# Fusing the layer-0 query, key and value units to 512 columns, with a new TensorE order, in a two-layer diffusion trunk

## The chip, the cores and the metric

The kernel runs on one core of one Trainium2 chip. The metric is the device time of one execution in microseconds (us); three executions of the kernel before gave a median of 1700.06 us, between 1699.44 and 1702.07.

## The reference, cut to what matters

The program is one inference step of a two-layer trunk. Layer 0 mixes tokens with differential attention, layer 1 with neighbourhood attention; each is followed by a squared-ReLU MLP. There are 128 context tokens and 512 latent tokens, 1024 features. The change touches only layer 0's mixer, which for the latent tokens is

```python
def diff_qkv(h, w_qkv):
    q, k, v = jnp.split(h @ w_qkv, 3, -1)        # 8 heads, each 2 x 64 of q and k, 128 of v
...
def diff_lat(h, ck, cv, w_qkv, lam, subln, w_o):
    q, k, v = diff_qkv(h, w_qkv)
    q, k = axial_rope(q), axial_rope(k)          # rotation, latent tokens only
    k_all = jnp.concatenate([ck, k], 1)          # 128 cached keys + 512 latent keys
    v_all = jnp.concatenate([cv, v], 1)
    # per head: p = softmax over 640 keys of two score maps; a = p0 - lam * p1; o = a @ v_all
    return diff_attend(q, k_all, v_all, diff_lambda(lam), subln) @ w_o
```

Context tokens do the same among themselves, without rotation. All matmuls of the projections are done in three passes of split numbers (high x high, low x high, high x low).

## The kernel before

Tokens are held in five tiles of 128 (`t` 0 to 3 latent, 4 context). The weights of the query, key and value projection lie in six chunks of 512 columns (chunk 0: v of heads 0 and 1, q and k of head 0; 1: q1 k1, v of heads 2 and 3; 2: q2 k2, q3 k3; 3: v of heads 4 and 5, q4 k4; 4: q5 k5, v of heads 6 and 7; 5: q6 k6, q7 k7). A chunk is four groups; a ring of five groups is kept in SBUF. When the last user of a group has run (`used`, `done`, the counts in `left`, L88 to L95), the next group is converted (`conv`: one ACT cast L194, two DVE subtractions L196) and a further load is issued on SP's queue (`pump`, three raw buffers, which also carry the modulation weights).

TensorE's instructions run in exactly the order of the string `ORDER0` (L40); the other engines are ordered by the compiler. Each name in it is one step:

- `q{i}{t}`, `v{i}{t}` (`unit0`, L525): the projection of one token tile to 256 columns: 8 k-tiles x 3 passes = 24 matmuls into one M bank (four PSUM banks M). `A` (`pair0`) does the q units of head 1 for two tiles together. `e{t}` takes head 0's parts out of the first stage's accumulators.
- `qk0_evac` (L481): takes a q unit out of PSUM. Latent tiles are rotated by four DVE instructions (L497 to L500) into a buffer `nt`, with a small ACT copy (L506). There are three buffers `nt` and one spare piece of the output tile `X`; the buffer is held until `r{i}{t}`. `v_evac` (L438): ACT cast and DVE subtraction (L126, L127) of a v unit.
- `r{i}{t}` (L515): three transposes of a buffer `nt`; ACT and DVE then write the queries (L517, L519) and keys (L518, L521). The queries have one buffer, so `r{i}{t}` comes after `S{i-1}{t}`.
- `S{h}{b}` (`scores0`): the scores of 128 queries of head h, 8 matmuls of 320 columns into two PSUM tiles S. There are just two such tiles; each is free again when its exponential has been taken. `softmax0`: per tile a DVE maximum (L570) and an ACT exponential (L572), then DVE L578 to L580 make one map E.
- `c{h}`: the context's scores, 4 matmuls, into one tile S, with the same softmax.
- `T{h}{b}` (L591): five transposes of E; at b = 1 a sixth, of the context's map (L593). `C{h}`, `P{h}`: the products with v (3 and 15 matmuls). `Q{h}` (L626): ten one-column matmuls for the mean square; after heads 3, 5, 6 and 7 a DVE and ACT chain of small instructions follows (`rstd0`, L637 to L646, with a table load for the square root), and `D3` and `D5` (L651) transpose its result.
- `m{g}`, `M{g}`: one modulation unit (8 weight tiles against the conditioning vector) and its two transposes.

```python
    def S(self):
        self.turn = (self.turn + 1) % len(self.psS)
        return self.psS[self.turn].tile([P, 1024], F32, tag="S", name=self.nm("S"))
...
        s2 = [self.S().rearrange("p (a b) -> p a b", b=512) for _ in range(2)]
        for hf in range(2):
            ks = slice(P + 320 * hf, P + 320 * hf + 320)
            self.qk([s2[m][:, hf, :320] for m in range(2)], self.q0, K, qs, lambda z: z[:, ks])
```

Of the kernel before, what the change touches and what calls it, by code (L numbers as in the profile page):

```python
# [39 lines left out]
ORDER0 = """  # L40
    e0 e4 A e2 v10 e1 m8 v13 b e3 r00 r04 q10 r02 q14 r01 q12 r03 m9 M8 S00 r10 v11 S01 r11 v12 c0 r14 v14 M9
    T00 S02 q21 q20 q30 r12 m10 T01 S03 r13 q23 m11 T02 S10 T03 r20 q31 C0 c1 M10 P0 m12 T10 S11 M11 r21 M12
    q22 S12 m13 q24 r22 T11 S13 r23 q32 r24 C1 T12 S20 r30 m14 M13 Q0 T13 M14 c2 P1 S21 T20 r31 q33 S22 T21
    q34 r32 Q1 S23 r33 v21 v20 r34 S30 T23 q40 v24 m15 T22 S32 C2 P2 m16 T30 r40 S31 q42 M16 q41 c3 r42 q43
    q44 T31 S33 r43 v22 r41 v23 M15 C3 r44 Q2 T32 q50 T33 S40 m17 P3 m18 S41 M18 q52 c4 Q3 T40 q51 v33 D3 r51
    r50 q53 M17 S42 v31 r52 q54 T41 S43 r54 r53 v30 S50 T43 v34 T42 v32 S51 q70 q61 C4 P4 c5 m19 T50 q60 m20
    M19 S52 r60 M20 q62 m21 r61 T52 q63 T51 S53 r62 M21 q64 r63 m22 r64 T53 C5 S60 M22 Q4 P5 S61 q71 m23 N2 c6
    Q5 M23 r70 q72 r71 T60 S62 D5 N1 T61 q73 N0 r72 q74 S63 N3 C6 T62 N4 N5 X r73 r74 o00 S70 T63 o02 c7 P6
    o03 T70 S71 Q6 o01 T71 D6 S72 o04 o10 T72 S73 C7 N6 o11 T73 o12 P7 o13 Q7 D7 o14 N7 j00 j10 j01 j11 g0 j12
    g1 j02 j13 h0 g2 j03 j04 h1 j14 g3 g4 h2 f0 f2 h3 f3 h4 f1  # L50
"""
# [14 lines left out]
class Net:  # L66
    def __init__(self, tc, a, o, stack):
# [22 lines left out]
        for l in range(2):  # L90
            for n in range(NCH):
                k = (9, 9, 8, 9, 9, 8)[n] if n < 6 and l else 10 if n < 6 else 8 if n > 7 and n % 4 < 2 else NTT
                for x in range(4):
                    self.left[4 * (NCH * l + n) + x] = k
# [17 lines left out]
    def op(self, name, fn, *needs):  # L112
        self.ops[name] = fn, needs
# [367 lines left out]
    def qk0_evac(self, pool, i, t, src):  # L481
        nc = self.nc
        if self.spare[1] not in self.ops:
            self.spare[1] = f"r{i}{t}"
            nt = self.spare[0][:, 0:384]
        else:
            nt = pool.tile([P, 384], F32, tag="nt", name=self.nm("nt"), bufs=3)
# [36 lines left out]

    def unit0(self, pool, kind, i, t, n, c):  # L525
        m = self.M()
        self.nat(self.h, t, n, m[:, :256], c, c + 256)
        if kind == "v":
            self.v_evac(pool, i, t, m[:, :256], "cv0", "v0")
        else:  # L530
            self.qk0_evac(pool, i, t, m[:, :256])

    def pair0(self, pool, ts):
        ms = [(t, self.M()[:, :256]) for t in ts]
        for k0, k1 in ((0, 6), (6, KT)):
            for t, m in ms:
                self.nat(self.h, t, 1, m, 0, 256, k0, k1, k0 == 0)
        for t, m in ms:
            self.qk0_evac(pool, 1, t, m)

# [132 lines left out]
    def layer0_attn(self, acc0):  # L673
        nc, a = self.nc, self.a
        with self.tc.tile_pool(name="at0", bufs=1) as pool:
# [5 lines left out]
            X = self.X([P, KT, NT])  # L681
            self.spare = [X[:, 6, :], "", ""]
            heads, norms, late = {}, {}, {}

# [53 lines left out]
            op("b", lambda: (self.banks("M", 4), self.lambdas(pool)), "e4")  # L738
            for kind, i, n, c in (
                ("q", 1, 1, 0), ("v", 1, 1, 256), ("q", 2, 2, 0), ("q", 3, 2, 256), ("v", 2, 3, 0), ("q", 4, 3, 256),  # L740
                ("q", 5, 4, 0), ("v", 3, 4, 256), ("q", 6, 5, 0), ("q", 7, 5, 256),
            ):
                for t in range(NTT):
                    if i == 1 and kind == "q" and t in A0:
                        continue
                    op(f"{kind}{i}{t}", lambda x=(kind, i, t, n, c): self.unit0(pool, *x))
            for g in range(KT, 24):
                op(f"m{g}", lambda g=g: self.mod_unit(pool, g))
            for h in range(8):
                rot = ("e",) if h == 0 else (f"q{h}",)  # L750
                for b in range(4):
                    op(f"S{h}{b}", lambda h=h, b=b: scores(h, b), *rot, f"r{h}")
                    op(f"T{h}{b}", lambda h=h, b=b: self.trans0(heads[h], b, b == 1), f"S{h}{b}", f"c{h}" if b == 1 else "-", f"T{h}0" if b else "-", f"P{h - 1}")
                op(f"c{h}", lambda h=h: self.ctx_scores0(heads[h]), *rot, f"r{h}", f"S{h}0")
                op(f"C{h}", lambda h=h: self.ctx_pv0(heads[h]), f"T{h}1", f"v{h // 2}4")
                op(f"P{h}", lambda h=h: pv(h), f"T{h}", f"v{h // 2}", f"C{h}")
                op(f"Q{h}", lambda h=h: ssq(h), f"P{h}")
                if h in (3, 5, 6, 7):
                    op(f"D{h}", lambda h=h: diag(h), *(f"Q{x}" for x in range(h + 1)))
                op(f"N{h}", lambda h=h: norm(h), f"D{max(h, 3 if h < 4 else 5)}", *(("X",) if h > 5 else ()))  # L760
            op("X", swap, "N0", "N1", "N2", "N3", "N4", "N5", "q", "v", "m", "M")
            first4 = self.proj_ops(pool, 0, late, EARLY0, "S73", ("N6", "N7"), ("E0", 2, "E1"))
# [638 lines left out]
```

## Time and profile before

| what | us |
|---|---|
| median of 3 executions | 1700.06 |
| the profiled execution | 1701.12 |
| its span in the profile | 1699.3 |
| layer 0's attention, from `A` (56.60) to `T50` (280.22) | 223.6 |
| TensorE busy, whole span | 1620.8 |
| VectorE busy, whole span | 1116.3 |
| ScalarE busy, whole span | 662.4 |

The profile's times are counted from the span's start. PE is the TensorE matmul, PEld its weight load, DVE VectorE, ACT ScalarE, POOL GpSimd, SP the queue that issues most transfers. In the timeline a row holds start, duration, engine, line of the kernel, operation, tile written <- tiles read, and in brackets the idle time of the engine just before it with what ended it. A matmul's duration includes its drain, so rows of PE overlap: what one matmul costs in a stream is the distance between two starts.

### The profile page before, as it was taken

To read this page: it belongs to the slowest core of one execution; us is meant where nothing else is said; L and a number is where in the kernel's file an instruction comes from. 1 tells how busy PE (TensorE), PEld (TensorE's weight loads), DVE (VectorE), ACT (ScalarE), POOL (GpSimd) and SP (SyncE) were. 2 spreads that over 40 slices of the span, in tenths; PEclk is the share of its full clock that TensorE was granted. 3 is DMA by queue.
4 is the path that set the end of the run, shared out by engine and by line. 5 is a ranking of instruction groups with operands and counts; after the bars stand their busy time and mean duration, and the time that the engine had idled before them with its cause. 6 is when DMAs were issued, how large, how long until landed. Compare 5 with 4: busy or idle time off the path is not lost. (4 is left out here: it accounts for less than half of the span.)

```text
span 1699.3 us, 25833 instructions
## 1 busy us (share of the span) xinstructions
PE 1620.8 (95%) x10026; PEld 1466.2 (86%) x10026; DVE 1116.3 (66%) x2121; ACT 662.4 (39%) x1338; POOL 370.3 (22%) x280
## 2 busy tenths in 40 slices
PE   8999999899999999999999999998899999999997
PEld 5788989787988988989888999997797898998996
DVE  4788778875668789798465777778655433242337
ACT  2466555743621221312335556565361122130321
POOL 2100000000062246164311001100015314334321
PEclk9999999999999999999999999999999999999999
DMA  8432334331424445353224443444042222122211
GB/s 335 131 133 93 100 116 151 112 130 40 162 86 149 161 137 185 125 186 124 88 86 160 126 126 119 148 149 168 15 148 74 79 71 85 65 85 65 89 61 62
DMA packets 61373, 200.73 MB, mean 118 GB/s; under 512 B 7764, under 2 KB 14402, under 8 KB 60226
## 3 DMA queue, kind: packets, MB, share of 16 engines
q1 hardware_dynamic: 55618, 175.09, 30.8%
q0 software_dynamic: 5632, 23.99, 4.1%
q8 instruction: 79, 1.29, 0.3%
q14 instruction: 44, 0.36, 0.1%
HBM read 186.41 MB, written 7.40 MB: 114 GB/s over the span
## 5 line engine op out<-in xcount | busy, mean ns | idle before, releaser
L194 ACT CAST wh<-rw 128x1024 fp32r<-128x1024 f32 x192 | 197.2, 1051 | 359.9 <-PE M L121 269.3
L121 PE MATMUL S<-hhi,wl 128*128 128x320 f32 (+1 forms) x944 | 292.7, 310 | 4.1 <-DVE wl L196 2.7
L119 PE MATMUL S<-hhi,wh 128*128 128x320 f32 (+1 forms) x944 | 292.0, 309 | 1.1 <-DVE tmp L1136 1.1
L120 PE MATMUL S<-hlo,wh 128*128 128x320 f32 (+1 forms) x944 | 291.5, 309 | 0.0
L196 DVE TENSOR_TENSOR wl<-rw,wh 128x512 fp32r<-128x512 f32 x278 | 247.9, 931 | 51.6 <-ACT wh L194 50.0
L196 POOL TENSOR_TENSOR wl<-rw,wh 128x512 fp32r<-128x512 f32 x106 | 182.2, 1738 | 405.7 <-ACT wh L194 404.1
L120 PE MATMUL M<-wl,uhi 128*128 128x512 f32 x640 | 252.2, 394 | 6.7 <-DVE wl L196 6.7
L119 PE MATMUL M<-wh,uhi 128*128 128x512 f32 x640 | 251.7, 393 | 1.8 <-ACT uhi L126 1.8
L121 PE MATMUL M<-wh,ulo 128*128 128x512 f32 x640 | 251.6, 393 | 0.3
L119 PE MATMUL M<-wh,hhi 128*128 128x256 f32 (+1 forms) x640 | 201.3, 314 | 8.2 <-DVE tmp L1136 3.2
L121 PE MATMUL M<-wh,hlo 128*128 128x256 f32 (+1 forms) x640 | 196.3, 307 | 5.2 <-DVE hlo L127 5.2
L120 PE MATMUL M<-wl,hhi 128*128 128x256 f32 (+1 forms) x640 | 195.6, 306 | 0.0
L121 PEld LDWEIGHTS S<-hhi,wl 128*128 128x128 f32 x944 | 178.4, 189 | 7.3 <-DVE wl L196 5.5
L119 PEld LDWEIGHTS S<-hhi,wh 128*128 128x128 f32 x944 | 178.5, 189 | 1.6 <-DVE tmp L1136 1.3
L120 PEld LDWEIGHTS S<-hlo,wh 128*128 128x128 f32 x944 | 178.4, 189 | 0.2
L120 PEld LDWEIGHTS M<-wl,uhi 128*128 128x128 f32 x640 | 121.4, 190 | 33.6 <-DVE wl L196 8.8
L119 PEld LDWEIGHTS M<-wh,uhi 128*128 128x128 f32 x640 | 121.4, 190 | 28.3 <-ACT uhi L126 3.6
L121 PEld LDWEIGHTS M<-wh,ulo 128*128 128x128 f32 x640 | 121.5, 190 | 26.9 <-DVE ulo L127 1.7
L293 DVE SCALAR_TENSOR_TENSOR jk<-wm,cb 128x1024 bf16<-128x1024 f32 x96 | 143.0, 1489 | 1.5
L119 PEld LDWEIGHTS M<-wh,hhi 128*128 128x128 f32 x640 | 124.1, 194 | 15.2 <-DVE tmp L1136 3.4
L121 PEld LDWEIGHTS M<-wh,hlo 128*128 128x128 f32 x640 | 123.6, 193 | 13.8 <-DVE hlo L127 9.3
L1195 DVE SCALAR_TENSOR_TENSOR r<-S,r 128x640 f32<-128x640 f32 (+1 forms) x62 | 48.4, 781 | 128.1 <-ACT r L1194 127.9
(278 smaller groups left out, 2958.7 us busy)
## 6 DMA issues: line engine op xcount, KB each, us to landing
rw<-in_w SPq DMA_DIRECT2D x192, 512.0 KB, 4.3
wm<-in_wmodT SPq DMA_DIRECT2D x48, 512.0 KB, 3.5
rw<-in_wmod SPq DMA_DIRECT2D x32, 512.0 KB, 4.4
E<-in_bias POOLq DMA_DIRECT2D x32, 384.0 KB, 5.4
wm<-in_wmod SPq DMA_DIRECT2D x8, 1024.0 KB, 10.7
Q<-Q SPq DMA_DIRECT2D x16, 320.0 KB, 4.1
gate<-gates POOLq DMA_DIRECT2D x6, 512.0 KB, 4.9
X<-in_xT SPq DMA_DIRECT2D x8, 320.0 KB, 11.4
```

Of the source, the lines that this page charges most:

```text
L119: te.matmul(out, sh, mh, start=start, stop=False)
L120: te.matmul(out, sh, ml, start=False, stop=False)
L121: te.matmul(out, sl, mh, start=False, stop=stop)
L194: keep(nc.scalar.copy(hi, r))
L196: keep(eng.tensor_tensor(lo[:, k], r[:, k], hi[:, k], ALU.subtract))
L293: op = nc.vector.scalar_tensor_tensor(jk, ws[t], 1.0, cb[:, x, :], ALU.mult, ALU.mult, accum_out=mc[:, t, x : x + 1])
L1195: nc.vector.scalar_tensor_tensor(rv, src, 0.0, rv, ALU.max, ALU.mult)
```

## The change

Query and value units that share a chunk become one unit of 512 columns: q1 with v1, q2 with q3, v2 with q4, q5 with v3, for each of the five token tiles; chunks 0 and 5 stay as they were. One M bank then holds both halves, and `evac0` takes them out one after the other. `A` computes 512 columns for tiles 1 and 3. Since head 3's rows are projected together with head 2's, long before they are transposed, their rotated rows are kept in three planes of the output tile `X` that are not yet in use (`nt3`) and not in the buffers `nt`. The counts of `left` follow (5 uses of a group in chunks 1 to 4). `ORDER0` is new up to `c5`; from `T50` on it is unchanged. The `v` names are gone from the rules. The diff:

```diff
--- before.py
+++ after.py
@@ -38,16 +38,15 @@
 HALF = (slice(0, 64), slice(64, 128))
 
 ORDER0 = """
-    e0 e4 A e2 v10 e1 m8 v13 b e3 r00 r04 q10 r02 q14 r01 q12 r03 m9 M8 S00 r10 v11 S01 r11 v12 c0 r14 v14 M9
-    T00 S02 q21 q20 q30 r12 m10 T01 S03 r13 q23 m11 T02 S10 T03 r20 q31 C0 c1 M10 P0 m12 T10 S11 M11 r21 M12
-    q22 S12 m13 q24 r22 T11 S13 r23 q32 r24 C1 T12 S20 r30 m14 M13 Q0 T13 M14 c2 P1 S21 T20 r31 q33 S22 T21
-    q34 r32 Q1 S23 r33 v21 v20 r34 S30 T23 q40 v24 m15 T22 S32 C2 P2 m16 T30 r40 S31 q42 M16 q41 c3 r42 q43
-    q44 T31 S33 r43 v22 r41 v23 M15 C3 r44 Q2 T32 q50 T33 S40 m17 P3 m18 S41 M18 q52 c4 Q3 T40 q51 v33 D3 r51
-    r50 q53 M17 S42 v31 r52 q54 T41 S43 r54 r53 v30 S50 T43 v34 T42 v32 S51 q70 q61 C4 P4 c5 m19 T50 q60 m20
-    M19 S52 r60 M20 q62 m21 r61 T52 q63 T51 S53 r62 M21 q64 r63 m22 r64 T53 C5 S60 M22 Q4 P5 S61 q71 m23 N2 c6
-    Q5 M23 r70 q72 r71 T60 S62 D5 N1 T61 q73 N0 r72 q74 S63 N3 C6 T62 N4 N5 X r73 r74 o00 S70 T63 o02 c7 P6
-    o03 T70 S71 Q6 o01 T71 D6 S72 o04 o10 T72 S73 C7 N6 o11 T73 o12 P7 o13 Q7 D7 o14 N7 j00 j10 j01 j11 g0 j12
-    g1 j02 j13 h0 g2 j03 j04 h1 j14 g3 g4 h2 f0 f2 h3 f3 h4 f1
+    e0 e4 A e2 e1 m8 b e3 r00 r04 q10 r02 r01 q14 r03 m9 M8 S00 r10 S01 r11 q12 c0 r14 M9 T00 S02 r12 q21 m10 T01
+    S03 r13 m11 T02 q20 S10 T03 r20 C0 c1 M10 P0 m12 T10 S11 M11 r21 M12 q22 S12 m13 T11 r22 q24 S13 r24 C1 T12 q23
+    Q0 m14 M13 T13 r23 S20 r30 M14 c2 P1 S21 T20 r31 q40 S22 T21 r32 Q1 S23 T22 r33 r34 q42 S30 T23 m15 C2 P2 m16
+    T30 r40 q41 S31 M16 c3 T31 r41 q43 S32 M15 r42 S33 C3 T32 q44 r43 Q2 T33 m17 r44 S40 P3 q50 m18 T40 S41 M18 r50
+    q51 c4 Q3 D3 T41 r51 S42 M17 q52 T42 r52 S43 q53 C4 r53 T43 q54 P4 m19 r54 S50 S51 q70 q61 c5 T50 q60 m20 M19
+    S52 r60 M20 q62 m21 r61 T52 q63 T51 S53 r62 M21 q64 r63 m22 r64 T53 C5 S60 M22 Q4 P5 S61 q71 m23 N2 c6 Q5 M23
+    r70 q72 r71 T60 S62 D5 N1 T61 q73 N0 r72 q74 S63 N3 C6 T62 N4 N5 X r73 r74 o00 S70 T63 o02 c7 P6 o03 T70 S71 Q6
+    o01 T71 D6 S72 o04 o10 T72 S73 C7 N6 o11 T73 o12 P7 o13 Q7 D7 o14 N7 j00 j10 j01 j11 g0 j12 g1 j02 j13 h0 g2 j03
+    j04 h1 j14 g3 g4 h2 f0 f2 h3 f3 h4 f1
 """
 ORDER1 = """
     e1 e3 e2 e0 b q03 v04 B00 q00 B03 q01 q02 q12 v11 S00 q10 B01 B02 c0 B10 q11 S01 v13 q13 B12 S02 T00 v12
@@ -89,7 +88,7 @@
         self.left = [0] * (8 * NCH)
         for l in range(2):
             for n in range(NCH):
-                k = (9, 9, 8, 9, 9, 8)[n] if n < 6 and l else 10 if n < 6 else 8 if n > 7 and n % 4 < 2 else NTT
+                k = ((10, 5, 5, 5, 5, 10), (9, 9, 8, 9, 9, 8))[l][n] if n < 6 else 8 if n > 7 and n % 4 < 2 else NTT
                 for x in range(4):
                     self.left[4 * (NCH * l + n) + x] = k
         self.left[: 4] = [NTT] * 4
@@ -480,7 +479,9 @@
 
     def qk0_evac(self, pool, i, t, src):
         nc = self.nc
-        if self.spare[1] not in self.ops:
+        if i == 3:
+            nt = self.nt3[:, 384 * t : 384 * t + 384]
+        elif self.spare[1] not in self.ops:
             self.spare[1] = f"r{i}{t}"
             nt = self.spare[0][:, 0:384]
         else:
@@ -522,21 +523,26 @@
 
         self.op(f"r{i}{t}", tr, f"S{i - 1}{t}" if t < 4 else f"c{i - 1}")
 
-    def unit0(self, pool, kind, i, t, n, c):
+    def unit0(self, pool, t, n, parts):
         m = self.M()
-        self.nat(self.h, t, n, m[:, :256], c, c + 256)
-        if kind == "v":
-            self.v_evac(pool, i, t, m[:, :256], "cv0", "v0")
-        else:
-            self.qk0_evac(pool, i, t, m[:, :256])
+        self.nat(self.h, t, n, m[:, : 256 * len(parts)], 256 * parts[0][2], 256 * parts[-1][2] + 256)
+        self.evac0(pool, t, m, parts)
+
+    def evac0(self, pool, t, m, parts):
+        for x, (kind, i, _) in enumerate(parts):
+            src = m[:, 256 * x : 256 * x + 256]
+            if kind == "v":
+                self.v_evac(pool, i, t, src, "cv0", "v0")
+            else:
+                self.qk0_evac(pool, i, t, src)
 
     def pair0(self, pool, ts):
-        ms = [(t, self.M()[:, :256]) for t in ts]
+        ms = [(t, self.M()) for t in ts]
         for k0, k1 in ((0, 6), (6, KT)):
             for t, m in ms:
-                self.nat(self.h, t, 1, m, 0, 256, k0, k1, k0 == 0)
+                self.nat(self.h, t, 1, m, 0, 512, k0, k1, k0 == 0)
         for t, m in ms:
-            self.qk0_evac(pool, 1, t, m)
+            self.evac0(pool, t, m, (("q", 1, 0), ("v", 1, 1)))
 
     def mod_unit(self, pool, g):
         acc = self.M()
@@ -680,6 +686,7 @@
             self.ssq = pool.tile([P, KT, NTT], F32, name="ssq")
             X = self.X([P, KT, NT])
             self.spare = [X[:, 6, :], "", ""]
+            self.nt3 = X[:, 3:6, :].rearrange("p a b -> p (a b)")
             heads, norms, late = {}, {}, {}
 
             def first(t):
@@ -736,29 +743,29 @@
                 op(f"e{t}", lambda t=t: first(t))
             op("A", lambda: self.pair0(pool, A0))
             op("b", lambda: (self.banks("M", 4), self.lambdas(pool)), "e4")
-            for kind, i, n, c in (
-                ("q", 1, 1, 0), ("v", 1, 1, 256), ("q", 2, 2, 0), ("q", 3, 2, 256), ("v", 2, 3, 0), ("q", 4, 3, 256),
-                ("q", 5, 4, 0), ("v", 3, 4, 256), ("q", 6, 5, 0), ("q", 7, 5, 256),
+            for i, n, parts in (
+                (1, 1, (("q", 1, 0), ("v", 1, 1))), (2, 2, (("q", 2, 0), ("q", 3, 1))), (4, 3, (("v", 2, 0), ("q", 4, 1))),
+                (5, 4, (("q", 5, 0), ("v", 3, 1))), (6, 5, (("q", 6, 0),)), (7, 5, (("q", 7, 1),)),
             ):
                 for t in range(NTT):
-                    if i == 1 and kind == "q" and t in A0:
+                    if i == 1 and t in A0:
                         continue
-                    op(f"{kind}{i}{t}", lambda x=(kind, i, t, n, c): self.unit0(pool, *x))
+                    op(f"q{i}{t}", lambda x=(t, n, parts): self.unit0(pool, *x))
             for g in range(KT, 24):
                 op(f"m{g}", lambda g=g: self.mod_unit(pool, g))
             for h in range(8):
-                rot = ("e",) if h == 0 else (f"q{h}",)
+                rot = ("e",) if h == 0 else (f"q{2 if h == 3 else h}",)
                 for b in range(4):
                     op(f"S{h}{b}", lambda h=h, b=b: scores(h, b), *rot, f"r{h}")
                     op(f"T{h}{b}", lambda h=h, b=b: self.trans0(heads[h], b, b == 1), f"S{h}{b}", f"c{h}" if b == 1 else "-", f"T{h}0" if b else "-", f"P{h - 1}")
                 op(f"c{h}", lambda h=h: self.ctx_scores0(heads[h]), *rot, f"r{h}", f"S{h}0")
-                op(f"C{h}", lambda h=h: self.ctx_pv0(heads[h]), f"T{h}1", f"v{h // 2}4")
-                op(f"P{h}", lambda h=h: pv(h), f"T{h}", f"v{h // 2}", f"C{h}")
+                op(f"C{h}", lambda h=h: self.ctx_pv0(heads[h]), f"T{h}1")
+                op(f"P{h}", lambda h=h: pv(h), f"T{h}", f"C{h}")
                 op(f"Q{h}", lambda h=h: ssq(h), f"P{h}")
                 if h in (3, 5, 6, 7):
                     op(f"D{h}", lambda h=h: diag(h), *(f"Q{x}" for x in range(h + 1)))
                 op(f"N{h}", lambda h=h: norm(h), f"D{max(h, 3 if h < 4 else 5)}", *(("X",) if h > 5 else ()))
-            op("X", swap, "N0", "N1", "N2", "N3", "N4", "N5", "q", "v", "m", "M")
+            op("X", swap, "N0", "N1", "N2", "N3", "N4", "N5", "q", "m", "M")
             first4 = self.proj_ops(pool, 0, late, EARLY0, "S73", ("N6", "N7"), ("E0", 2, "E1"))
             self.run(ORDER0)
             return late["X"], first4
```

## The prediction

> **What bounds the kernel now.** I read the page first, then busy time by windows, then TensorE's waits in the stage that the change touches, then its timeline step by step against `ORDER0`.
>
> ```profile
> PE 1620.8 (95%) x10026; PEld 1466.2 (86%) x10026; DVE 1116.3 (66%) x2121; ACT 662.4 (39%) x1338; POOL 370.3 (22%) x280
> ```
> ```profile
> 56.60:99.76 43.16, 39.85 (x334) 37.18 (x332) 34.93 (x103) 24.14 (x66) 1.82 (x4) 1.00 0.39 129
> 99.76:280.22 180.46, 175.97 (x1415) 162.05 (x1415) 145.46 (x381) 103.41 (x270) 7.62 (x14) 0.99 0.34 113
> ```
> ```profile
> PE M L119 <- DVE red L270: 2.2, 1, 2.2
> PE M L591 <- DVE E L580: 1.3, 2, 1.0
> PE M L591 <- DVE V L127: 1.1, 1, 1.1
> PE M L515 <- DVE V L127: 0.9, 1, 0.9
> ```
>
> From `A` (56.60) to `T50` (280.22) TensorE is busy 216 of 224 us, and and the four longest kinds of wait come to 5.5 of the other 8. DVE is busy 180 of 224, 81%. The stage is a TensorE stream whose order leaves every softmax time to end beneath other matmuls. So two questions decide: what TensorE saves, and whether the new order still covers the softmax. Both orders hold the same steps up to `T50`, so the two can be compared there.
>
> **The saving.** A 256-column unit and 512-column runs, by their first row and the first row behind them:
>
> ```profile
> 88.54 0.36 PE L119 MATMUL M<-wh,hhi 128*128 128x256 f32 x1
> 91.50 0.22 PE L455 MATMUL S<-K,q 128*128 128x128 f32 x1
> ```
> ```profile
> 362.19 0.47 PE L119 MATMUL M<-wh,hhi 128*128 128x512 f32 x1
> 366.40 0.71 PE L591 MATMUL M<-idf,E 128*128 128x128 f32 x5
> 368.23 0.40 PE L119 MATMUL M<-wh,hhi 128*128 128x512 f32 x1
> 376.41 0.71 PE L591 MATMUL M<-idf,E 128*128 128x128 f32 x5
> ```
>
> The unit costs 2.96 us for 24 matmuls. The runs are three quarters of a unit (18 matmuls, 4.21 us) and one and a half (36, 8.18), so a whole one is 5.61 or 5.45; I take 5.53. Forty units of 2.96 (118.4) become twenty of 5.53 (110.6): 7.8 us saved, 6.2 to 9.4 by the two runs. Evacuations, transposes, conversions and loads keep their number, so nothing else is saved. Per matmul pair the rows give 2 x 123 - 230 = 16 ns, and I go by them. The Trainium skill (TensorE: Matmul & The Clock Gate, section Back-to-back issue gap) has N/2.4 + 2.5 ns for a matmul of N columns; by that a pair would save 2.5 ns, 480 pairs 1.2 us.
>
> **The waits that the new order makes.** Two tiles S serve all scores. Here are a fast and an ordinary score pass, each from the first TensorE row behind it, then two context passes:
>
> ```profile
> 231.78 0.38 PE L268 MATMUL M<-idf,rows 128*128 128x128 f32 x2
> 232.55 0.80 ACT L572 ACTIVATE E<-S,mx 128x640 f32<-128x640 f32 x1 [1.25 <-DVE mx L570]
> 233.33 0.79 ACT L572 ACTIVATE E<-S,mx 128x640 f32<-128x640 f32 x1
> 234.69 0.89 DVE L580 SCALAR_TENSOR_TENSOR E<-E,c,E 128x640 f32<-128x640 f32 x1
> ```
> ```profile
> 117.89 0.71 PE L591 MATMUL M<-idf,E 128*128 128x128 f32 x5
> 119.43 0.81 ACT L572 ACTIVATE E<-S,mx 128x640 f32<-128x640 f32 x1
> 120.20 0.81 ACT L572 ACTIVATE E<-S,mx 128x640 f32<-128x640 f32 x1
> 121.81 0.88 DVE L580 SCALAR_TENSOR_TENSOR E<-E,c,E 128x640 f32<-128x640 f32 x1
> ```
> ```profile
> 279.22 1.07 PE L259 MATMUL M<-rw,sc 128*32 128x256 f32 x16
> 280.99 0.37 ACT L572 ACTIVATE E<-S,mx 128x128 f32<-128x128 f32 x1
> 281.94 0.35 DVE L580 SCALAR_TENSOR_TENSOR E<-E,c,E 128x128 f32<-128x128 f32 x1
> ```
> ```profile
> 235.27 1.23 PE L626 MATMUL M<-mean,sq 128*128 128x1 f32 x10
> 238.57 0.37 ACT L572 ACTIVATE E<-S,mx 128x128 f32<-128x128 f32 x1 [0.24 <-DVE mx L570]
> 239.51 0.35 DVE L580 SCALAR_TENSOR_TENSOR E<-E,c,E 128x128 f32<-128x128 f32 x1
> 236.35 0.74 PE L591 MATMUL M<-idf,E 128*128 128x128 f32 x5
> ```
>
> After a score pass the first tile is free at 1.6 (fast) to 2.4 us, the second at 2.3 to 3.1, the map E is ready at 3.8 to 4.8. After a context pass the tile is free at 2.1 to 3.7, its map ready at 3.1 to 4.6. These are the two ends for each wait below; DVE's queue makes the difference. A second score pass whose second tile comes free at e, after x us of other work, is late by e - 0.3 - x: its first two of eight matmuls need only the first tile, and the other six end 0.9 behind e where the whole pass takes 1.2. Of work between, `T` counts 0.55, `r` 0.25, `M` 0.15, `C` 0.3, `c` 0.45, `Q` 1.1 (235.27 to 236.35), as the timeline spaces their first rows.
>
> The old order has always a unit or a P between two passes. The new one has:
> - `S00 r10 S01`: x = 0.25, late by 1.8 to 2.6; I take 2.0.
> - `c0 r14 M9 T00 S02`: x = 0.95, 0.9 to 2.4; 1.3. This takes the place of the 2.2 before `q21` in the list of waits.
> - `S10 T03 r20 C0 c1`: the first tile, x = 1.1: 0.5 to 1.3; 0.7.
> - `S20 r30 M14 c2`: x = 0.4: 1.2 to 2.0; 1.4.
> - `S22 T21 r32 Q1 S23 T22`: x = 1.9, 0.2 to 1.0; then `T22` wants S22's map, 0.6 to 0.8: together 1.0.
> - `S31 M16 c3 T31`: c3 has x = 0.15 and waits 1.4 to 2.2. `T31` then needs S31's map and c3's. c3 ends at 2.0 to 2.8, its map is there 3.1 to 4.6 later, and of that T31 fills about 0.5: 2.6 to 4.1. I take 1.7 + 3.0.
> - `S32 M15 r42 S33 C3 T32`: x = 0.4: 1.7 to 2.4; T32 0.3 to 0.5. Together 2.2.
> - `S50 S51`: x = 0: 2.0 to 2.8; 2.2.
>
> That is 15.5 us. Behind each waiting instruction stands all the rest of TensorE's stream, the next unit first; ACT and DVE, which would evacuate that unit, wait for it in turn.
>
> Two waits are of another kind. `r02 r01` now stand together. `e1` gets its buffer only from r02, since r04, r11 and r13 hold the three (e4, and both tiles of `A`, come first):
>
> ```profile
> 73.96 0.49 PE L515 MATMUL M<-idf,nt 128*128 128x128 f32 x3
> 76.36 0.30 ACT L506 COPY nt<-nt 128x128 f32<-128x128 f32 x1 [0.35 <-DVE nt L500]
> ```
>
> From r02's end (74.45) to the end of the rotation (76.66) are 2.2 us, which q14 used to cover and now nothing does: 2.2 (1.9 to 2.5). `c4 Q3 D3`: D3 used to come 6.3 us behind Q3, with T40 and two units between:
>
> ```profile
> 236.75 0.15 DVE L627 COPY ssq<-M 128x5 f32<-128x5 f32 x1
> 239.04 1.28 ACT L640 ACT_TABLE_LOAD   x1
> 241.91 0.18 DVE L646 TENSOR_TENSOR ssq<-ht,ht 128x20 f32<-128x20 f32 x1
> ```
>
> The chain ends at 242.09, 5.7 us after Q3 (236.35). With empty queues it would be 0.55 to the copy's end, 1.5 for table and square root, some 1.6 for eight small DVE instructions: 3.7. The table load stands behind c4's exponentials on ACT, the small ones behind q51's rotation on DVE, so I take 4.4. Last, `r23 S20`: the second half of the scores needs r23's keys.
>
> ```profile
> 83.92 0.49 PE L515 MATMUL M<-idf,X 128*128 128x128 f32 x3
> 85.69 0.59 DVE L521 TENSOR_TENSOR K<-M,K 64x128 fp32r<-64x128 f32 x2
> ```
>
> That took 1.9 us from the transposes' end (84.41 to 86.28), of which 0.6 is covered: 0 to 1.5; 0.7. All waits: 15.5 + 2.2 + 4.4 + 0.7 = 22.8, between 19 with all fast ends and 32 with the ordinary ones.
>
> **The clock.** Waits have a second price:
>
> ```profile
> 214.90:218.29 3.39, 1.95 (x15) 1.72 (x15) 3.34 (x9) 0.96 (x5) 0.00 (x0) 1.00 0.54 176
> 218.30:221.70 3.40, 2.99 (x14) 2.94 (x14) 2.58 (x7) 1.58 (x3) 0.00 (x0) 0.50 0.91 294
> ```
> ```profile
> 218.79 0.55 PE L119 MATMUL M<-wh,hhi 128*128 128x256 f32 x1 [0.41 <-DVE K L521]
> 223.02 0.71 PE L591 MATMUL M<-idf,E 128*128 128x128 f32 x5
> ```
>
> After 3.4 us with only 1.95 busy the granted clock was 0.50 for 3.4 us, and a unit took 4.23 us for 2.96: 1.3 lost. I count three such stretches (r01 or S01, T31, D3): 3.9, between none and six (7.8). Gaps of 1.1 and 0.4 with ten one-column matmuls before them sufficed. The Trainium skill (the same page, section Why this matters for your kernels) warns only of idle gaps above about 3 us; by that only T31 and D3 would do it, 2.6 for 3.9, and the sum would be 1.3 lower.
>
> **What goes, and what costs nothing.** The 2.2 before q21 and 1.0 of T23's wait (T23 now has q42 and S30 before it) go; of the waits of 1.1 and 0.4 and the slow unit (1.3) between 215 and 223 I let half go (1.4), since conversions now spread over longer units, and 0.7 of the smaller ones: 5.3, bounds 2.2 to 7.5. Moving head 3's rotation earlier only adds four DVE instructions to each q2 unit, where 5.5 us of matmuls cover them. The two halves share a bank:
>
> ```profile
> 75.64 0.37 ACT L126 CAST V<-S 128x256 fp32r<-128x256 f32 x1 [0.50 <-DVE t L499]
> ```
>
> ACT's cast of a v half waits for the rotation's third instruction on the same tile; what queues behind it on ACT are exponentials, and S waits for those. The Trainium skill (PSUM — Partial Sum Buffer, section PSUM bank collisions raise a hardware error) says that no two engines may touch one bank at once, which speaks against this change; the row agrees. Fifteen such units at up to 0.5 are covered by the unit of matmuls behind them, except in front of the waits above, where they push to the ordinary ends. In the load queue m14 now stands behind q23, so two of three raw buffers are taken when chunk 3's groups are wanted. Each of two groups then takes some 7 us of load and conversion in series; between q23 and q40's second half lie about 20 us, so I cost it at nothing.
>
> **The sum.** -7.8 + 22.8 + 3.9 - 5.3 = +13.6 on the profiled execution's 1701.1 (its span of 1699.3 and 1.8 around it), so 1714.7; that execution stood 1.1 above the median of the three, so against the median it is 1713.6. With all ends low (waits 19, no slow clock, 9.4 and 7.5 off) it is +2; with all high (32 + 7.8 - 6.2 - 2.2) it is +31.
>
> **The rivals.**
> (1) Faster: DVE stays shorter than the fast ends, since while TensorE waits no new evacuation arrives; the score waits vanish, and just r01 and D3 remain (2.2 + 4.4). Then -7.8 - 5.3 + 6.6 = -6.5: 1693.6. For it speaks DVE's 81%; against it, that maximum and two exponentials in series cannot end in 0.25 us. It decides where the score waits and slow stretches sum below 6. Chance 0.10.
> (2) No change: all low ends and no slow clock, 1702. Chance 0.13, as six low ends must meet.
> (3) Fusing saves next to nothing: a 256-column matmul's 123 ns would be nearly all streaming, a wide unit would cost 5.86 us, and of the 7.8 only 1.2 would be left: 1713.6 + 6.6 = 1720. The rows at 88.54 and 368.23 speak against it; 0.05. It is what the Trainium skill's gap, above, would make of it.
> (4) Weights late: ACT stands at a cast whose load hasn't landed, in front of q40, and exponentials behind it; some 6 us more, a group's 7 less what is spare, and two more slow stretches, 1722. 0.06.
> The forecast itself has the remaining 0.66.
>
> **The numbers.** 1713.6 us. The range is 1699 to 1725: the low end leaves out most of rival 1, the high end the upper third between forecast and +31. About 0.2%, 3.4 us, is what a measurement of this kernel can tell from no change: faster 0.10, the same 0.13, slower 0.77.
>
> **What would show it.** Rows of 512 columns in units of about 5.5 us; waits of TensorE on `ACT E L572` (S tiles) and `DVE E L580` (maps), now 0.2 and 1.3 us in this stage, summing above 10; a wait before L651 of about 4 us; a wait of L515 on ACT L506 or DVE in the first 25 us; more stretches of clock 0.50 before 280. `T50` should come some 14 us later than 280.22. I am wrong if the waits in front of S, c and T stay below 5 us together, or if T50 comes earlier while its units cost what I say.

## The result, and the profile after

| | before | after |
|---|---|---|
| median, us | 1700.93 (4 runs) | 1757.39 (4 runs, 1755.16 to 1759.92) |
| ratio to before | 1 | 1.0335, 95% interval 1.0322 to 1.0349 |
| profiled span, us; mean clock | 1699.3; 0.983 | 1754.1; 0.968 |

The change makes the kernel slower by 56 us. The forecast said slower by 14; 1757 lies far above its range.

Busy time by windows, after (first the stage from `A` to `T50`, then the rest), and the same of before. Columns: window, length, then busy time and instructions of PE, PEld, DVE, ACT, POOL, then granted clock, DMA share, GB/s.

```profile
57.01:335.49 278.48, 231.14 (x1270) 186.94 (x1268) 182.94 (x479) 127.48 (x335) 8.83 (x18) 0.90 0.29 97
335.49:1754.10 1418.61, 1358.13 (x7986) 1235.22 (x7985) 909.73 (x1587) 516.66 (x976) 347.47 (x242) 0.98 0.33 111
```
```profile
56.60:280.22 223.62, 215.82 (x1749) 199.23 (x1747) 180.39 (x483) 127.55 (x335) 9.44 (x18) 0.99 0.35 116
280.22:1699.30 1419.08, 1357.15 (x7988) 1233.66 (x7984) 908.31 (x1582) 516.94 (x977) 346.94 (x242) 0.98 0.34 112
```

The rest is the same length in both (1418.6 and 1419.1). All of the loss is in the stage: 278.5 against 223.6, 54.9 us. VectorE and ScalarE do much the same work as before (183 and 127 us against 180 and 128), so no engine became the bound; TensorE stands more, and its clock fell from 0.99 to 0.90. TensorE's waits in the stage, after (total, times, longest):

```profile
PE S L454 <- ACT E L578: 10.3, 10, 1.9
PE M L258 <- DMA rw<-in_wmod: 6.8, 3, 3.0
PE S L454 <- DVE K L522: 5.5, 3, 3.6
PE M L516 <- ACT X L507: 5.0, 3, 2.7
PE M L657 <- DVE ssq L652: 4.0, 1, 4.0
PE M L597 <- DVE V L126: 3.8, 1, 3.8
PE M L516 <- ACT nt L507: 2.8, 2, 2.0
PE M L597 <- DVE E L586: 2.6, 2, 1.8
```

With the smaller ones these are 46.9 us; before they were 7.2. Read step by step against `ORDER0`, the 54.9 us divide so: steps undisturbed and at full clock -7.5; waits +39.7; matmuls stretched by half clock +21.1 (22.7 against 1.6); small rest +1.6. The three parts without the waits make 15.2, and the windows above show 15.3 more of TensorE's busy time.

The clock. One stretch and the one in front of it, then three more, after:

```profile
89.06:92.46 3.40, 1.74 (x10) 1.48 (x11) 2.72 (x8) 2.16 (x6) 0.00 (x0) 1.00 0.85 311
92.46:95.87 3.41, 3.41 (x11) 2.73 (x10) 2.87 (x6) 2.09 (x6) 0.91 (x2) 0.51 0.07 21
```
```profile
252.88:259.69 6.81, 4.61 (x26) 2.95 (x27) 2.05 (x6) 1.04 (x4) 0.00 (x0) 0.50 0.71 244
280.16:286.97 6.81, 3.70 (x17) 3.73 (x18) 3.87 (x17) 3.80 (x10) 0.72 (x1) 0.51 0.01 2
317.76:331.40 13.64, 11.38 (x53) 9.04 (x54) 5.54 (x11) 4.76 (x12) 1.06 (x2) 0.50 0.45 162
```

Where TensorE was busy for only 1.74 of 3.40 us (two waits at S01, 1.25 and 0.49), the next 3.41 ran at 0.51, though TensorE was then busy throughout. The stage has sixteen such lengths of 3.4 us, 54.6 us in all, in seven stretches of one to four lengths; before it had one length. The busy time of a length alone does not decide what follows. Of the lengths at full clock, those with 1.5 us busy or less were all followed by half clock. Between 1.6 and 2.0 the outcome was mixed: 1.74 was followed by half clock, 1.62, 1.64, 1.71 and 1.94 were not. With more than 2.0 busy just one was followed by half clock, the one in front of the row at 280.16, which holds `Q3`'s ten one-column matmuls. After:

```profile
276.75:280.16 3.41, 2.56 (x19) 2.28 (x18) 2.21 (x9) 1.19 (x6) 0.00 (x0) 1.00 0.00 0
304.09:307.50 3.41, 1.71 (x12) 1.57 (x13) 1.98 (x5) 1.42 (x5) 0.00 (x0) 1.00 0.00 0
307.50:310.91 3.41, 3.41 (x17) 2.79 (x16) 2.87 (x7) 2.29 (x4) 0.00 (x0) 1.00 0.03 7
```

Each stretch of this stage went on after a slow length with 2.83 us busy or less and ended with the first slow length in which TensorE was busy throughout.

Two of the waits were priced far too low or not at all. First `S20`: TensorE's rows, then ACT and DVE, after.

```profile
172.73 0.60 PE L454 MATMUL S<-K,q 128*128 128x320 f32 x1 [3.64 <-DVE K L522]
...
175.03 0.60 PE L454 MATMUL S<-K,q 128*128 128x320 f32 x1 [1.44 <-DVE K L522]
```
```profile
169.90 1.04 ACT L193 CAST wh<-rw 128x1024 fp32r<-128x1024 f32 x1 [0.60 <-DMA rw<-in_w]
172.19 1.04 ACT L193 CAST wh<-rw 128x1024 fp32r<-128x1024 f32 x1 [1.25 <-DMA rw<-in_w]
```
```profile
170.97 1.29 DVE L195 TENSOR_TENSOR wl<-rw,wh 128x512 fp32r<-128x512 f32 x2 [0.74 <-ACT wh L193]
172.30 0.28 DVE L522 TENSOR_TENSOR K<-M,K 64x128 fp32r<-64x128 f32 x1
173.27 1.29 DVE L195 TENSOR_TENSOR wl<-rw,wh 128x512 fp32r<-128x512 f32 x2 [0.69 <-ACT wh L193]
174.59 0.29 DVE L522 TENSOR_TENSOR K<-M,K 64x128 fp32r<-64x128 f32 x1
```

The keys of r23 take 0.28 us each, and on VectorE each runs behind a weight conversion, which waits for a cast, which waits for a load. So a late load in the weight queue stops scores that need no new weight. The same kind of queue stands before `T00`, whose last block needs a PSUM bank that q12's value half still holds:

```profile
105.01 0.30 PE L597 MATMUL M<-idf,E 128*128 128x128 f32 x1 [3.79 <-DVE V L126]
```
```profile
99.06 2.49 DVE L195 TENSOR_TENSOR wl<-rw,wh 128x512 fp32r<-128x512 f32 x4
...
102.90 1.29 DVE L195 TENSOR_TENSOR wl<-rw,wh 128x512 fp32r<-128x512 f32 x2 [0.50 <-ACT wh L193]
104.11 0.42 DVE L501 TENSOR_TENSOR X<-X,t 128x256 f32<-128x256 f32 x1
104.45 0.42 DVE L126 TENSOR_TENSOR V<-M,V 128x256 fp32r<-128x256 f32 x1
```

### The profile page after: what moved, and what is told of

Read it like the earlier page. It is cut to its first block, busy times and chain, and to the rows that moved or that the text cites. A ratio compares the mean times of both kernels' runs of the same rounds, so it can differ in the third digit from the quotient of the medians.

```text
span 1754.1 us, 24873 instructions
## 1 busy us (share of the span) xinstructions
PE 1637.4 (93%) x9546; PEld 1455.8 (83%) x9546; DVE 1120.3 (64%) x2121; ACT 661.9 (38%) x1338; POOL 370.3 (21%) x280
## 4 chain that ended last, share of the span: by engine, by line
PE 66%; DVE 11%; issue 6%; ACT 3%; DMA 2%; POOL 1%; DVEq 0%; POOLq 0%; ACTq 0%; SPq 0%
PE M L120 12%; PE M L118 12%; PE M L119 12%; PE S L120 7%; PE S L118 7%; PE S L119 7%; DVE wl L195 4%; PE S L454 1%; PE S L455 1%; ACT wh L193 1%; DMA X<-rnd 1%; DMA rw<-in_wmod 1%; POOL wl L195 1%; PE M L861 1%; DVE hlo L126 1%
## 5 line engine op out<-in xcount | busy, mean ns | idle before, releaser
L195 DVE TENSOR_TENSOR wl<-rw,wh 128x512 fp32r<-128x512 f32 x278 | 248.6, 934 | 54.9 <-ACT wh L193 53.0
L118 PE MATMUL M<-wh,hhi 128*128 128x512 f32 (+1 forms) x480 | 175.2, 365 | 8.3 <-DVE tmp L1143 3.2
L120 PE MATMUL M<-wh,hlo 128*128 128x512 f32 (+1 forms) x480 | 171.3, 357 | 5.5 <-DVE hlo L126 5.3
L119 PE MATMUL M<-wl,hhi 128*128 128x512 f32 (+1 forms) x480 | 170.8, 356 | 0.0
L1094 DVE TENSOR_TENSOR tmp<-M,gate 128x512 f32<-128x512 f32 x80 | 54.9, 686 | 114.3 <-PE M L120 113.1
L120 PEld LDWEIGHTS M<-wh,hlo 128*128 128x128 f32 x480 | 94.9, 198 | 21.2 <-DVE hlo L126 9.7
```

Source lines behind the costliest of these rows:

```text
L118: te.matmul(out, sh, mh, start=start, stop=False)
L119: te.matmul(out, sh, ml, start=False, stop=False)
L120: te.matmul(out, sl, mh, start=False, stop=stop)
L195: keep(eng.tensor_tensor(lo[:, k], r[:, k], hi[:, k], ALU.subtract))
L1094: nc.vector.tensor_tensor(tmp, m, gate[t // 4][:, cs], ALU.mult)
```

## The experiments

Times are medians beside the kernel before on the same chip (1699.8 to 1701.0). Stage is `A` to `T50` in each profile, with its mean granted clock.

| kernel | us | ratio, 95% | stage, us | clock |
|---|---|---|---|---|
| before | | 1 | 223.6 | 0.99 |
| after | 1757.4 | 1.0322 to 1.0349 | 278.5 | 0.90 |
| e1_narrow | 1752.8 | 1.0258 to 1.0325 | 273.1 | 0.94 |
| e2_loads | 1750.2 | 1.0247 to 1.0311 | 276.6 | 0.90 |
| e3_old | 1744.0 | 1.0207 to 1.0276 | 263.5 | 0.90 |
| e4_warm | 1754.2 | 1.0301 to 1.0332 | 275.3 | 0.95 |
| e5_fix | 1731.9 | 1.0134 to 1.0203 | 256.4 | 0.94 |
| e6_fixnarrow | 1727.6 | 1.0146 to 1.0176 | 252.1 | 0.95 |
| f1_pair1 | 1710.2 | 1.0036 to 1.0068 | 231.7 | 0.98 |
| f2_pair23 | 1716.0 | 1.0072 to 1.0102 | 237.4 | 0.95 |
| f3_pair3 | 1709.6 | 1.0028 to 1.0065 | 232.8 | 0.96 |
| f4_pair4 | 1710.7 | 1.0033 to 1.0067 | 232.8 | 0.98 |
| g1_d3 | 1706.4 | 1.0024 to 1.0047 | 232.2 | 0.98 |
| h1_d3back | 1757.2 | 1.0303 to 1.0351 | 280.1 | 0.90 |
| i1_pool1 | 1759.8 | 1.0311 to 1.0355 | 283.4 | 0.89 |
| i2_pool2 | 1762.9 | 1.0342 to 1.0373 | 285.4 | 0.89 |
| i3_before_pool1 | 1703.3 | 1.0005 to 1.0026 | 226.8 | 0.98 |
| i5_pair1_pool1 | 1717.7 | 1.0075 to 1.0109 | 241.8 | 0.94 |

**Width or order: e1_narrow, e3_old.** The theory: the order loses the time, as steps that separated short ones are gone. The rival: the wide unit does, by its 5.5 us and by two evacuations on one bank. First the new order with narrow units (the edit in `unit0`; `A` and the counts of `left` follow it):

```
-        self.nat(self.h, t, n, m[:, : 256 * len(parts)], 256 * parts[0][2], 256 * parts[-1][2] + 256)
-        self.evac0(pool, t, m, parts)
+        for part in parts:
+            m, c = self.M(), 256 * part[2]
+            self.nat(self.h, t, n, m[:, :256], c, c + 256)
+            self.evac0(pool, t, m, (part,))
```


> The new order, but each wide unit is computed as its two halves of 256 columns in a row, each in a bank of its own; head 3's rows still wait in the output tile. Order theory (the 55 us are waits at short distances in the new order, and the slow clock that follows them): the waits stay, and the 7.5 us that fusing saves are lost, so about 1757 + 7 = 1764, between 1755 and 1770. Fusion theory (the waits come from the wide units themselves, by the shared bank and blocks of 5.5 us): most of the waits go, under 1725.

Measured 1752.8, just below the expected 1755 to 1770 and far above the fusion theory's 1725: the waits come with the order. The 7.5 us that the narrow units cost more in matmuls do not appear: TensorE's waits are 43.0 us for 46.9 (T00 2.03 for 3.79), and nine lengths at half clock stand for sixteen, which pays for them. So in this order fusing saves nothing that could be measured.

Then wide units in the old order, at the places of q1, q2, q4 and q5, without the names v1, v2, v3 and q3 (shown against the order of before):

```
-    e0 e4 A e2 v10 e1 m8 v13 b e3 r00 r04 q10 r02 q14 r01 q12 r03 m9 M8 S00 r10 v11 S01 r11 v12 c0 r14 v14 M9 ...
+    e0 e4 A e2 e1 m8 b e3 r00 r04 q10 r02 q14 r01 q12 r03 m9 M8 S00 r10 S01 r11 c0 r14 M9 ...
```


> The wide units, in the order of before with the names of the v and q3 units just left out; nothing else moved. Order theory: distances are as short as in the new order or shorter at S22, S30, T43 and D3, so the time is between 1735 and 1775, with waits on exponentials and maps. Rival (the new order is at fault for itself, the old one would have carried the wide units): 1693 to 1705.

Measured 1744.0, as the order theory has it. The old order too loses 44 us once its twenty separating units are gone. The new order is 13 us worse still than that.

**One chunk at a time: f1, f2, f3, f4.** Each is the kernel before with one chunk's units fused; the names of the other half (v1, q3, v2 or v3) go from the old order. The cut is condensed: it holds for the one chunk alone, and `parts` are its two halves.

```
-                    op(f"{kind}{i}{t}", lambda x=(kind, i, t, n, c): self.unit0(pool, *x))
+                    op(f"{kind}{i}{t}", lambda x=(t, n, parts): self.wide0(pool, *x))
+    def wide0(self, pool, t, n, parts):
+        m = self.M()
+        self.nat(self.h, t, n, m, 0, 512)
+        self.evac0(pool, t, m, parts)
```


> The kernel before with another part of the change alone: only the queries of head 1 and the values of heads 2 and 3 come in units of 512 columns, at the old places of head 1's queries (two of them in A); the places of the values are empty, all else stays in the old order. Spacing theory: v11, v12 and v14 stood between S01 and c0; in the old order without all twenty separating units c0 waited 7.2 us there, with a half-clock stretch of 10.2 us behind it (5.1 us lost), and about 2 us come back by fusing: 1706 to 1714. Rival, the other chunks made that wait: 1697 to 1702.

> The kernel before with one part of the change alone: only the queries of heads 2 and 3 come in units of 512 columns, at the old places of head 2's units; the five places of head 3's units are empty, its rows wait in the output tile; all else is in the old order. Spacing theory: five of twenty separating units are gone, a quarter of the 44 us that the old order lost without all twenty, less or more by place: 1704 to 1716. Fusing theory (wide units save 0.37 us each, the old order covers the rest): 1696 to 1700.

> The kernel before with chunk 3 alone fused (values of heads 4 and 5 with the queries of head 4, at the old places of the latter). Spacing theory: the five places v20 to v24 stand between the first scores of head 3 and T32; in the old order without all twenty units S30 waited 2.0 us there and the steps up to T32 about 3 us more, with half clock behind them: 1702 to 1710. If the four parts add up to the 44 us of all four together, this one and the next two share 28. Fusing theory: 1697 to 1700.

> The kernel before with chunk 4 alone fused (queries of head 5 with the values of heads 6 and 7, at the old places of the former). The values are due only after head 5, so these five separate the second half of head 4's steps and the first of head 5's without being due. Spacing theory: in the old order without all twenty units r51, r53, S50 and S51 waited 7 us together and a half-clock stretch of 6.8 us followed: 1706 to 1714. Fusing theory: 1697 to 1700.

Measured +9.4, +15.8, +8.8 and +9.9 against before on the same chip, each within the range of the spacing theory: 43.9 together, and all four at once (e3_old) gave 44.3. The costs add, so each chunk pays for its own five empty places, and no chunk of the four can be fused at a gain at these places. Where it is paid is local. TensorE at `c0` in f1_pair1, then VectorE there:

```profile
103.46 0.47 PE L454 MATMUL S<-K,q 128*128 128x128 f32 x1 [6.86 <-ACT E L583]
```
```profile
96.43 2.85 DVE L195 TENSOR_TENSOR wl<-rw,wh 128x512 fp32r<-128x512 f32 x4
...
100.60 0.41 DVE L126 TENSOR_TENSOR V<-M,V 128x256 fp32r<-128x256 f32 x1
101.04 0.59 DVE L522 TENSOR_TENSOR K<-M,K 64x128 fp32r<-64x128 f32 x2
101.66 1.55 DVE L581 TENSOR_REDUCE mx<-S 128x1 f32<-128x640 f32 x2
```

c0 waits for a score tile of S01. S01's maxima come only at 101.66, behind four conversions and the whole evacuation of a wide unit. In the old order v11, v12 and v14 were TensorE's work around these steps.

**One step moved: g1_d3, h1_d3back.** In before D3 goes directly behind Q3; in after it goes back behind q52.

```
-  ... Q3 T40 q51 v33 D3 ...
+  ... Q3 D3 T40 q51 v33 ...
```


> The kernel before with one step moved: D3 directly behind Q3, as the change has it, instead of three steps later. All units stay at 256 columns. Wait-and-clock theory: TensorE waits 4 us for VectorE's sums as in the changed kernel (3.96 us), and a half-clock stretch of 3.4 to 6.8 us follows, 1.7 to 3.4 us more: 1703 to 1709. Rival, the work behind covers the wait (the units that follow ran into waits anyway): 1699 to 1702.


```
-  ... Q3 D3 T41 r51 S42 M17 q52 ...
+  ... Q3 T41 r51 S42 M17 q52 D3 ...
```


> The changed kernel with one step moved back: D3 stands behind q52 instead of directly behind Q3. If a wait costs its length and the half-clock stretch behind it, as in the kernel before (6 us for this one step), 1749 to 1753 us. Rival: in the changed order the time is taken by the next waits (r52, r53, m19, S51), as with the filled waits: 1754 to 1758.

TensorE at D3 in g1_d3, and the clock behind it:

```profile
239.52 0.39 PE L650 MATMUL M<-idf,ssq 128*20 128x128 f32 x1 [4.15 <-DVE ssq L645]
```
```profile
237.57:244.38 6.81, 4.86 (x23) 4.86 (x24) 2.24 (x9) 1.39 (x4) 0.72 (x1) 0.50 0.13 41
```

Measured 6.2 us, for a wait of 4.15 and a half-clock stretch of 6.81 (1.9 us lost in it). Alone, a wait costs itself and then the clock. The way back in the changed kernel gave 1757.2, in the rival's range and no difference within some 3 us. The wait at D3 went, T41 waited 2.0 in its place, and from S40 to T50 the profile is 4.1 us shorter; from A to S40, with the same instructions in the same order, that execution was 5.7 us longer (206.4 against 200.7), with more stretches at half clock. So this run decides nothing.

**Loads: e2_loads.** The groups m14, m11, m17, m19 go to where their loads fall due as in the old order.

```
-  T12 q23 Q0 m14 M13   r13 m11 T02 q20 S10   T33 m17 r44 S40 P3 q50   P4 m19 r54 S50 S51 q70 q61 c5 T50
+  T12 m14 q23 Q0 M13   r13 T02 q20 m11 S10   T33 r44 S40 P3 m17 q50   P4 r54 S50 S51 q70 q61 c5 m19 T50
```


> The new order with four modulation units moved: m14 in front of q23, m11 behind q20, m17 behind P3, m19 behind c5. Load theory (m11, m17 and m19 stand right behind their loads, and m14 behind q23 holds two raw buffers when chunk 3 is wanted): the waits of 6.8 us on loads and some 5 us at S20 go, with three stretches of slow clock, so 1757 - 6.8 - 5 - about 10 = 1735. Rival (something else in the queues is as late): the same steps wait for DVE or ACT, over 1750.

Measured 1750.2, at the rival's end. The waits on loads are gone (6.8 us), the keys of S20 too (5.1 to 0.5), but T13 now waits 3.7 for VectorE's sums, and half clock grew. Of some 11 us of waits removed, 7 arrived in the median, a third of the 22 that the load theory had, and only 1.9 in the stage of the profiled execution.

**The clock: e4_warm.**

```
+    def warm(self, out, n):
+        for _ in range(n):
+            self.nc.tensor.matmul(out[:, :P], self.idf, self.ones, start=True, stop=True)
 called on the waiting step's own tile: D3 14, r01 7, r52 6, r53 9, m11 3, m17 10, m19 9
```


> The changed kernel with 58 extra multiplications of 128x128 that compute nothing, put into seven places where TensorE stood (14 before D3, 7 before r01, 6 before r52, 9 before r53, 3, 10 and 9 before m11, m17 and m19): they write the tile that the waiting step then overwrites, so its result stays the same. Clock theory: a wait of 2 to 4 us costs its length and then a stretch at half clock, because TensorE stood. With the waits filled the half-clock stretches that began at 252.9, 280.2 and 317.8 us (6.8 + 6.8 + 13.7 us, so 13.7 us of lost work) shrink or go, the waits themselves stay: 1742 to 1750 us. Rival: the half clock has another cause than the standing still, and the stretches stay: 1755 to 1762.

The half-clock stretches at 252.9 and 280.2 went and that at 317.8 shrank from 13.7 to 3.4 us; the clock in the stage rose:

```profile
56.59:331.89 275.30, 236.58 (x1385) 194.18 (x1384) 183.22 (x479) 127.84 (x335) 8.68 (x18) 0.95 0.30 98
```

So at these places standing brought the half clock, and 9.4 of the 22.7 us came back. But the time fell only by 3 us, to 1754.2, between the two expected ranges, and its interval overlaps that of after. At the seven places waits of 17.3 us became 14.3 us of filling and 6.3 us of waits, and other waits grew by 2.5: TensorE reached the next wait earlier, and its end was set by VectorE, ScalarE and loads. I read this as half clock in front of a wait being partly hidden by that wait.

**Other spacings: e5_fix, e6_fixnarrow.** The steps up to T50 in a third order that puts the wide units between the scores (its beginning below), and the same with narrow halves.

```
-  ... T00 S02 r12 q21 m10 T01 S03 r13 m11 T02 q20 S10 T03 r20 C0 c1 ...
+  ... T00 q20 S02 r12 m10 T01 S03 r13 T02 q22 m11 S10 T03 r20 m12 C0 c1 ...
```


> The wide units in an order of my own: between two score passes, and between a pass and its transposition, stands at least a unit, a P or about 2 us of small steps wherever the steps suffice; rotations have a step or more before their r, D3 stands behind q52, and m14, m17, m19 are moved as in the run above. Order theory: the waits fall from 47 to 10 to 18 us and most slow stretches go, so 1690 to 1712. Fusion theory (twenty wide units are too few to keep the passes apart whatever the order): over 1725.

> The re-spaced order (1731.9 us with wide units) with every wide unit computed as two units of 256 columns, back to back, each with its own bank. Order theory: the two halves stand at the same place, so the same steps wait, and only the 5 to 7 us of the separate matmuls come back or the bank gains offset them: 1727 to 1740. Rival, the wide unit (its 5.5 us block and the two evacuations that hold one bank) made the 32 us that this order still lost: under 1715.

1731.9 and 1727.6. The order alone is worth 25 us, which makes it the largest lever; it misses the 1690 to 1712 that I expected of it and lies where the rival had it, as 30.4 us of waits stayed where 10 to 18 were expected (S01 2.98, r54 2.18; r00 too waited 3.27, but the steps up to r00 are those of after, where it waited 1.32, and in e2_loads it waited 2.00). That this is not the width, e6 tells: with narrow halves the same order is no faster by more than these intervals can tell, and the rival (under 1715) is out. Fusing gains nothing measurable here either.

**VectorE's queue: i1, i2, i3, i5.** If conversions ahead of short instructions make the waits, GpSimd should take them.

```
-        for k, eng in enumerate([(nc.vector, nc.gpsimd)[x < self.pool_lo] for x in (1, 0)]):
+        for k, eng in enumerate([(nc.vector, nc.gpsimd)[x < (1 if 8 <= g < 24 else self.pool_lo)] for x in (1, 0)]):
```
(2 for 1 in i2_pool2.)

> The changed kernel; of each weight group of layer 0's chunks 2 to 5 the first half's low part is computed on GpSimd (3% busy in this stage) instead of VectorE, the second half stays. Queue theory: steps wait because short VectorE instructions (keys at 172.30 and 174.59, the V evacuation at 104.45) stand behind conversions of 1.3 to 2.5 us; half of that goes, about 4 of the 9 us before S20 and T00, 2 to 4 of the waits on maxima, and some half clock: 1742 to 1752 us. Rival, late loads and the length of each chain set the waits, whatever engine converts, and GpSimd is slower at a half (1.74 us elsewhere in this kernel): 1755 to 1765.

> As the run before, with both low halves on GpSimd, so VectorE's queue holds no conversion of chunks 2 to 5 at all. Queue theory: 1735 to 1748, less than with one half. Rival: a group then takes 3.5 us on GpSimd, four groups 14 us per chunk, and units wait for weights: over 1757.

> The kernel before with the same one half on GpSimd, as control. The queue's short instructions are covered there by the separate units: 1697 to 1702 by both theories. Above 1704 it would say that GpSimd's work itself costs (a slower chain, or VectorE slowed beside it), and the two runs before would have to be read against it.

> The kernel with chunk 1 alone fused (1710.2 us) and the same one half on GpSimd. There c0 waited 6.86 us, because the maxima of S01 stood on VectorE at 101.66 behind four conversions (96.43 to 99.3) and the evacuation of the wide unit behind these. Queue theory: of the four two remain, the maxima come some 1.5 to 2.5 us earlier, c0 waits 4 to 5.5: 1706 to 1709. Rival (the two evacuations of the wide unit, not the conversions, hold the maxima back): c0 waits 6.5 or more, 1709 to 1712.

None was faster: 1759.8, 1762.9, 1703.3, 1717.7. The control i3 lost 2 us too, more than both theories had and less than the 1704 that was to speak against GpSimd's work itself; i5 lies above both of its ranges, with eight lengths at half clock where f1_pair1 had three. As a remedy the queue theory fell. As a cause it has support: with no conversion of these chunks on VectorE, in i2_pool2, T00 waits 0.82 us (3.79 in after) and S20 for keys 1.11 (5.08). With half of them, in i1_pool1, S20's keys cost 2.38, but T00 still waited 3.80, then by the profile for another VectorE instruction.

```profile
109.05 0.30 PE L597 MATMUL M<-idf,E 128*128 128x128 f32 x1 [0.82 <-DVE V L126]
...
177.56 0.42 PE L454 MATMUL S<-K,q 128*128 128x320 f32 x1 [1.11 <-DVE K L522]
```

In i2_pool2 the time came back elsewhere: waits of modulation groups on loads rose from 6.8 to 11.6 us, and r00's from 1.32 to 4.2, though r00's differs among executions anyway. That a slower conversion holds the raw buffer longer would explain the loads; no run tests it. And VectorE was held up while GpSimd computed. From i5_pair1_pool1, VectorE, then GpSimd at the same time:

```profile
89.76 1.56 DVE L501 TENSOR_TENSOR X<-X,t 128x256 f32<-128x256 f32 x1
...
102.08 1.88 DVE L591 SCALAR_TENSOR_TENSOR E<-E,c,E 128x640 f32<-128x640 f32 x1
```
```profile
89.75 1.29 POOL L195 TENSOR_TENSOR wl<-rw,wh 128x512 fp32r<-128x512 f32 x1 [19.09 <-DVE K L522]
...
102.01 1.27 POOL L195 TENSOR_TENSOR wl<-rw,wh 128x512 fp32r<-128x512 f32 x1 [0.20 <-ACT wh L193]
```

The first took 0.42 in the row of L501 above, the second 0.89 in the first score pass that the prediction shows. The Trainium skill (Advanced Engine Details and Errata, section GPSIMD Details) says that Pool and DVE share a read and a write interface and conflict where a DVE instruction has two inputs in SBUF; both these have, and the rows agree. It went the other way where VectorE had begun first: beside its conversion at 97.61, which took the usual 0.69, GpSimd's took 1.78. c0 waited 5.67 for 6.86: less, but not the 4 to 5.5 expected. What part of c0's wait the conversions make, and what part the wide evacuation, stays open.

## Why the prediction was wrong, step by step

Right in sign and in its main mechanism, wrong in size: 13.6 forecast on the profiled execution, 54.9 in the stage. Two steps failed. Waits were put at nothing that came to 20.6 us, with one at 0.7 that came to 5.08; and half clock was put at 3.9 us and came to 22.7.

- **The saving** was of the right size: -7.8 forecast, -7.5 found. A unit by two rows of after (q14, and r03 behind it):

```profile
79.34 0.48 PE L118 MATMUL M<-wh,hhi 128*128 128x512 f32 x1
...
84.92 0.49 PE L516 MATMUL M<-idf,nt 128*128 128x128 f32 x3
```

  5.58 us here, 5.47 for most, 5.53 forecast. Rival 3 is out.
- **The waits that the order makes** were right as far as they were listed: 15.5 for scores and maps, found 13.1 (S01 1.74, S02 1.27, c1 none, c2 0.82, S23 and T22 1.82, c3 and T31 3.88, S33 2.14, S51 1.44); r01 2.2, found 2.03; D3 4.4, found 3.96. S02's 1.27 for 1.3 is luck: T00 in front of it had already waited 3.79, but c0's score tile came free not 2.1 to 3.7 but 6.6 us behind c0, since its maxima stood behind the same queue as T00's bank (104.78 and 106.03 on VectorE). Rival 1 (they vanish) and rival 2 are out.
- **S20 on r23's keys** was mis-sized: 0.7 forecast, 5.08 found. It was priced by the chain with a free VectorE; found was the chain behind two conversions.
- **What costs nothing** failed. "in front of the waits above, where they push to the ordinary ends" and "I cost it at nothing" left out: T00 3.79, the loads of m11, m17 and m19 6.8, r52 and r53 behind their rotations 4.6, and q23, q42, T33, r20 and P2 5.4. That is 20.6, with S20's 4.4 25 us. The rotations r52 and r53 were an oversight: only one other step stands between each and its unit, and the list was searched for scores. Rival 4 named the mechanism (a cast that waits for its load, and others queued behind) and let it end at q40; it ended at S20 by way of VectorE. As a case it was right in kind beside the forecast; that its price of some 6 is near S20's 5.08 is luck, as the path was another.
- **The clock** failed in number and length: three stretches of one length each, 3.9 us, bound 7.8; found seven stretches, sixteen lengths in all, and 22.7 us of stretched matmuls. The price of a length was right (1.4 against 1.3). The three that were named came (S01, T31, D3). Four more came with the waits that were not priced or priced too low (T00, S20, m17, m19), and six of the seven held on for more than one length, since TensorE stood again in the slow one. The sentence that the prediction takes from the Trainium skill, by which only gaps above 3 us count, would have made it worse, and the trace does not agree with it: the stretch after S01 came from waits of 1.25 and 0.49, while r53's wait of 2.71, in the row at 304.09, brought none. Another section of the same page (A second HAM failure mode: psum-queue depth-cycling) tells of short idles between groups of matmuls that make the clock go to and fro, and the row at 89.06 agrees with that. By e4_warm not all of the 22.7 us is a price of its own.
- **What goes** was about right: 5.3 forecast, bounds 2.2 to 7.5; of the 7.2 us of old waits only r00's 0.9 remains (1.32 now).

The runs show what stood behind both failures. A fused unit is due when the earlier of its halves is. The five freed places of a chunk were TensorE's work where VectorE and ScalarE then keep it waiting for up to 2 to 7 us at a step, and 9 to 16 us per chunk is the price by f1 to f4, after the 1.9 us that five units save. I had priced the places where two score steps meet, not all places that lost their cover. The further 13 us or so of the new order over the old one without those units are seen in its profile only as other waits (D3, r01, loads, r52, r53, against c0 of the old order); no single run settles their shares, and h1_d3back shows that the shares of one step are below what a run of this order can tell.

## What to carry to other kernels

Fewer, longer matmul steps save little when each also was the cover of another engine's chain: before fusing, list for every place that becomes empty what waits there, on scores, keys, evacuations and loads alike, and price the queue of the releasing engine, not its chain alone. A queue makes strangers wait for each other, so look for what stands ahead of a short instruction. Where several small waits fall into a few microseconds, count a half-clock stretch, longer if more waits follow, but expect it to be partly hidden under the next wait.

## What the runs showed of the hardware

- Half clock came in stretches of 3.4 us or multiples of it. Lengths of 3.4 us with 1.5 us busy or less were all followed by one in this stage; around half busy it went either way (1.74 was, 1.71 was not).
- GpSimd's conversions slowed VectorE beside them: an instruction of 0.42 us took 1.56, one of 0.89 took 1.88 (i5_pair1_pool1).
- The same instructions in the same order took 200.7 and 206.4 us from A to S40 in two executions, the second with more lengths at half clock; so in this order one execution says little of a few us.
